# Output projection of a hybrid encoder step: three row tiles in turn, one tile for turned rows, and rows asked for earlier

## The chip, the cores and the metric

One core of one Trainium2 chip runs the whole program. The metric is the time of one execution on the device in microseconds; of several runs the median is given. A profile is one further execution, taken by the hardware profiler.

## The reference, cut to what matters

The program is one inference step of a two-layer encoder over 2048 prompt rows and 32 sample rows of width 1024. The first layer is a gated delta rule, the second attends with shared keys and values. The change lies in the end of the first layer: the output projection, the residual sum and the layer norm.

```python
o = o * lax.rsqrt(jnp.mean(o * o, -1, keepdims=True) + RMS_EPS) * norm_w * jax.nn.silu(z.astype(jnp.float32))
out = o.reshape(b, l, A_VW).astype(x.dtype) @ w_out          # (2080 rows, 1024) @ (1024, 1024)
return layer_norm(DN_ALPHA * x + out, ln_g, ln_b), new_buf, s_new.astype(x.dtype)
```

All of it is computed to float32 accuracy: each operand of a matmul is split into a rounded part and a remainder (`_hi` and `_lo`), and three products are summed.

## The kernel before

**Tiling.** The output projection (`O1.tiles`, with `OutNorm` for the arithmetic) goes over 17 tiles of rows: 14 of 128 prompt rows, the 32 sample rows, and the last two of 128. For each tile the gated output `g` is read turned (128 x 8 x 128), split into `g_hi` (ScalarE, ACT) and `g_lo` (VectorE, DVE), and multiplied by the whole weight matrix, which stays in the on-chip memory as `wo_hi` and `wo_lo`. The two halves of 512 columns are c = 0 (PSUM bank `po`) and c = 1 (bank `ps`). For each half, after 24 matmuls, `add_products` (L1165) computes r = ALPHA * r + bank on DVE, where r holds the tile's 128 rows of the input x, and the statistics for the layer norm follow (L1226).

**The order inside a tile.** `OutNorm.tile` is a generator that stops after every six matmuls, eight times a tile: j = 0 to 3 in the first half, j = 4 to 7 in the second. `O1.tiles` puts work of the tile before, and preparations for the tiles to come, at these stops:

- j = 0: the mean and the inverse root of the tile before (`scaled`, a row of small DVE instructions down to `nb`, L1238);
- j = 1: its normalisation on ACT (L1239), `g_lo` of the next tile (L1209), and the load of `g` for the tile after that (L1187), whose one buffer is free when `g_lo` has been made;
- j = 3: the multiplication by ln_g and the addition of ln_b (L1243, L1244), and the store of the finished rows to the scratch array h (`s_h`, L1261);
- then the first half's update of r from `po`, which is emitted when the generator goes on;
- j = 4: the finished rows of the tile before are turned in blocks of 32 x 32 by DVE (L1267) into a tile `hT`, which four DMAs store to the scratch array (`s_hT`, L1270), each with 1024 pieces of 32 elements;
- j = 6: the load of the next tile's rows of x into r (L1192);
- after j = 7 the second half's update of r, from `ps`.

Between the stops a second generator (`more`) issues work of the next stage: loads of its weights (L1389) and of turned rows (L1367), partial sums on GpSimd (POOL) and their stores (L1432).

**What sets the order.** In this part the order on TensorE (PE), DVE, ACT and SP is that of the program text (`manual_schedule`). All loads and stores named here are issued by SP, one after another; an issue that has to wait holds up the issues behind it. A tile from a pool with two buffers may be written again when the readers of the tile before last are done.

**The buffers that matter.** r comes from the pool `two` of `OutNorm` (two buffers). `hT` comes from the pool `o1_hT` on the right side (two buffers of 128 x 1024 float32), opened when the delta rule is finished; the first tile still takes a buffer of the delta rule. `last.close()` gives that pool back after the last tile, and the next stage's `first_pair` places five tiles of activations (L1412) from there on.

**The next stage** (`P2`) multiplies the normalised rows by the weights of the second layer. Its first seven weight tiles are multiplied singly, in part between the last tiles of the projection; then follow groups of products over partial sums, which need the stored `hT` and the sums.

Of the kernel before, what the change touches and what calls it, by code (L numbers as in the profile page):

```python
# [11 lines left out]
F32 = mybir.dt.float32  # L12
# [9 lines left out]
D = 1024  # L22
# [14 lines left out]
def new_pool(tc, es, name, bufs=1, space=None, side=None):  # L37
    kw = {"reuse_waits": "tile"}
    if side is not None:
        kw["side"] = side  # L40
    if space is not None:
        kw["space"] = space
    return es.enter_context(tc.tile_pool(name=name, bufs=bufs, **kw))
# [1128 lines left out]
class OutNorm:  # L1172
# [15 lines left out]
        return g  # L1188

    def rows(self, src, n):  # L1190
        r = self.two.tile([128, D], F32, tag="r", name="r")
        self.queue.dma_start(r[:n], src)  # L1192
        return r

    spare = None

    def bank(self, c):
        if c and self.spare:
# [48 lines left out]
class O1:  # L1247
# [25 lines left out]
    def tiles(self, tiles, ready, more):  # L1273


        on, last, parts, beside = self.on, None, [], ()
        for t in tiles[:2]:
            while not ready(t):
                yield 1.0
            g = self.fetch(*t)  # L1280
            yield 0.0
            parts.append(on.low(g, on.cast(g, t[2]), t[2]))
        r = self.rows(*tiles[0])
        yield 0.0
        high, coming = None, ()
        for i, t in enumerate(tiles):
            beside = itertools.chain(beside, more(i))
            if i + 1 == len(tiles):
                yield from (out for out in beside if out)
            for j, out in enumerate(on.tile(parts.pop(0), r, t[2])):  # L1290
                yield out
                next(beside, None)
                if j == 0 and last:
                    normalise = on.scaled(*last)
                elif j == 1:
                    if last:
                        normalise()
                    for c in coming:
                        parts.append(on.low(g, high, c[2]))
                    coming = tiles[i + 2:i + 3]  # L1300
                    for c in coming:
                        while not ready(c):
                            yield 1.0
                        g = self.fetch(*c)
                elif j == 3 and last:
                    self.affine(last, *tiles[i - 1])
                elif j == 4 and last:
                    self.turned(last[0], *tiles[i - 1])
                if j == 6 and i + 1 < len(tiles):
                    following = self.rows(*tiles[i + 1])  # L1310
            for c in coming:
                high = on.cast(g, c[2])
            last, r = (r, t[2], on.stats), following
        end = more(len(tiles))
        normalise = on.scaled(*last)
        yield from itertools.islice(end, 2)
        normalise()
        self.affine(last, *tiles[-1])
        yield from itertools.islice(end, 2)
        self.turned(last[0], *tiles[-1])  # L1320
        yield from end


class P2:
# [249 lines left out]
    def plan(self, first, between, late, late_ps):  # L1574


        def singles(tiles, ps):
            return [p for i in tiles for p in self.single(i, ps)]

        one, a = self.groups(0)  # L1580
        two, b = self.groups(1)
        between = singles(between, self.ps)
        last = singles([self.Z + 1], self.ps)
        for n in a:
            self.then(a[n], self.operand(1, a[n].act[1]))
        early = [*singles(first, self.ps), *one, between[0], a["P4"], a["P3"], *between[1:], *two, last[0], b["P4"],
                 b["P3"], last[1]]
        late = singles(late, late_ps)
        self.main = self.stream(early + late, len(early) - 4)
        self.left = 2 * len(early)  # L1590
# [82 lines left out]
    now, later, side, beside = 0, (), iter(()), iter(())  # L1673
# [634 lines left out]
def program(tc, I, O, T, G):  # L2308
    nc = tc.nc
    left, right, mid = ExitStack(), ExitStack(), ExitStack()  # L2310
# [36 lines left out]
    o1 = []  # L2347
# [12 lines left out]
    def outputs():  # L2360
        tiles = [(t * 128, t * 128, min(128, NT - t * 128)) for t in (*range(14), NTT - 1, 14, 15)]
        yield from o1[0].tiles(tiles, lambda t: t[0] in sent, more)
# [27 lines left out]
    front, spare = ExitStack(), ExitStack()  # L2390
    p2.append(P2(tc, right, front, spare, I, O, T, G))
    last = ExitStack()
    hp = new_pool(tc, last, "o1_hT", 2, side="right")
    o1[0].room = lambda: hp.tile([128, KC, 128], F32, tag="hT", name="hT")[:]
    o1[0].on.spare = p2[0].ps
    later = []
# [218 lines left out]
```

## Time and profile before

| | us |
|---|---|
| runs shown (three) | 2056.74, 2059.09, 2065.05 |
| median | 2059.09 |
| profiled execution, whole time | 2061.92 |
| profiled execution, span of the page | 2060.1 |
| output projection in it (loads and tails included), about | 1061 to 1301 |

The span runs from the first instruction to the last; a little more lies around it. Times in the rows are microseconds from the start of the span. Engines: PE = TensorE matmul, PEld = TensorE weight load, DVE = VectorE, ACT = ScalarE, POOL = GpSimd, SP = SyncE (SPq: an issue on its queue). L1165 is line 1165 of the kernel. Matmuls overlap in the records: one lasts 0.39 us and the next begins 0.23 us after it. An idle time in brackets is that of the engine just before the instruction, with what ended it by the profile; a wait for several things is put down to the one that came last.

### The profile page before, as it was taken

How to read it: one execution, taken by the hardware profiler on the slowest of the kernel's cores; microseconds unless marked ns; L12 is line 12 of the kernel's file. 1: busy time of each engine (PE TensorE's matmuls, PEld its weight loads, DVE VectorE, ACT ScalarE, POOL GpSimd, SP SyncE). 2: the span in 40 equal slices, each digit the busy share in tenths (PEclk: the TensorE clock that was granted, in tenths of full speed). 3: DMA queues.
4: the chain of work that ended last, by engine and by line, in shares of the span. 5: the costliest groups of instructions: out<-in, count | busy, mean ns of one | idle time of the engine just before them, and what ended most of it. 6: DMA issues, size and time to landing. Idle time of an engine off the chain costs nothing. (4 is left out here: it accounts for less than half of the span.)

```text
span 2060.1 us, 36519 instructions
## 1 busy us (share of the span) xinstructions
PE 1999.7 (97%) x13246; PEld 1829.3 (89%) x13246; DVE 1477.9 (72%) x2701; ACT 999.0 (48%) x2437; POOL 740.9 (36%) x1151
## 2 busy tenths in 40 slices
PE   8999999999999999999889999899999999999998
PEld 6999999999999989999888887799999997777775
DVE  4677656677665778888987898787777755666665
ACT  4354443436632277777773222533643435555552
POOL 0212112121213258888760114022000014566665
PEclk9999999999999999999999999999999999999999
DMA  5133255447878466665885998888768579433321
GB/s 211 51 124 118 76 125 120 104 103 205 206 168 240 149 207 216 195 202 193 297 281 137 257 247 247 271 270 300 265 196 251 190 218 322 121 103 103 103 74 67
DMA packets 477076, 377.85 MB, mean 183 GB/s; under 512 B 291024, under 2 KB 397808, under 8 KB 476880
## 3 DMA queue, kind: packets, MB, share of 16 engines
q1 hardware_dynamic: 470416, 361.08, 59.4%
q10 hardware_dynamic: 6480, 14.44, 2.0%
q8 instruction: 104, 1.70, 0.3%
q14 instruction: 76, 0.62, 0.1%
HBM read 244.06 MB, written 142.58 MB: 188 GB/s over the span
## 5 line engine op out<-in xcount | busy, mean ns | idle before, releaser
L79 PE MATMUL ps<-act_hi,w_hi 128*128 128x416 f32 x1280 | 455.6, 356 | 3.7 <-DVE z L579 3.7
L81 PE MATMUL ps<-act_hi,w_lo 128*128 128x416 f32 x1280 | 450.5, 353 | 0.0
L80 PE MATMUL ps<-act_lo,w_hi 128*128 128x416 f32 x1280 | 448.8, 351 | 0.0
L79 PEld LDWEIGHTS ps<-act_hi,w_hi 128*128 128x128 f32 x1280 | 240.6, 188 | 8.5 <-DVE z L579 4.0
L81 PEld LDWEIGHTS ps<-act_hi,w_lo 128*128 128x128 f32 x1280 | 240.6, 188 | 3.8
L80 PEld LDWEIGHTS ps<-act_lo,w_hi 128*128 128x128 f32 x1280 | 241.2, 188 | 3.0
L212 DVE SCALAR_TENSOR_TENSOR y<-R,convw,y 128x2083 f32<-128x2083 f32 x72 | 177.7, 2469 | 56.9 <-ACT y L209 52.6
L755 POOL TENSOR_TENSOR tm<-L,Tt 128x60 f32<-128x60 f32 (+19 forms) x365 | 134.9, 370 | 74.4 <-issue 43.2
L56 POOL TENSOR_TENSOR w_lo<-w_raw,w_hi 128x1024 fp32r<-128x1024 f32 x25 | 62.6, 2503 | 273.1 <-ACT w_hi L55 273.1
L1881 ACT ACTIVATE e<-S,nm 128x193 f32<-128x193 f32 (+2 forms) x260 | 104.6, 415 | 102.5 <-DVE nm L1876 61.5
L757 POOL TENSOR_TENSOR Tt<-Tt,tm 128x60 f32<-128x60 f32 (+19 forms) x365 | 139.8, 383 | 28.6
L1895 POOL TENSOR_TENSOR P<-e,sm 128x384 f32<-128x384 f32 (+2 forms) x128 | 102.3, 820 | 119.0 <-DVE sm L1885 113.0
L326 ACT COPY R<-ps 128x416 f32<-128x416 f32 (+1 forms) x144 | 59.6, 445 | 125.5 <-PE ps L81 119.9
L1538 ACT ACTIVATE o<-X 128x416 f32<-128x416 f32 x80 | 41.4, 518 | 151.2 <-PE X L1712 147.8
L1383 POOL TENSOR_TENSOR wo_parts<-wo_parts 128x512 fp32r<-128x512 f32 x16 | 21.6, 1352 | 239.3 <-ACT wo_parts L1699 239.3
L1157 PE MATMUL ot<-wo,g_hi 128*128 128x512 f32 x256 | 103.7, 405 | 0.0
L1158 PE MATMUL ot<-wo,g_hi 128*128 128x512 f32 x256 | 100.8, 394 | 0.0
L1159 PE MATMUL ot<-wo,g_lo 128*128 128x512 f32 x256 | 100.8, 394 | 0.0
L1383 DVE TENSOR_TENSOR w_lo<-w_raw,w_hi 128x512 fp32r<-128x512 f32 x134 | 95.9, 730 | 4.3 <-ACT w_hi L1395 2.6
L1426 POOL TENSOR_TENSOR act_raw<-act_raw 128x416 f32<-128x416 f32 x32 | 41.7, 1303 | 134.1 <-DMA act_raw<-s_hT 132.4
L218 DVE SCALAR_TENSOR_TENSOR y<-th,y 128x2083 f32<-128x2083 f32 x24 | 55.8, 2327 | 31.5 <-ACT th L216 31.5
L1395 ACT CAST w_hi<-w_raw 128x512 fp32r<-128x512 f32 x129 | 76.1, 615 | 1.4 <-PE ps L1711 1.4
(368 smaller groups left out, 5086.8 us busy)
## 6 DMA issues: line engine op xcount, KB each, us to landing
w_raw<-in_b_w SPq DMA_DIRECT2D x60, 512.0 KB
w_raw<-in_w_in SPq DMA_DIRECT2D x40, 512.0 KB
act_raw<-s_hT SPq DMA_DIRECT2D x64, 208.0 KB
s_rows<-o SPq DMA_DIRECT2D x50, 208.0 KB
k<-s_k SPq DMA_DIRECT2D x17, 512.0 KB
E<-s_E SPq DMA_DIRECT2D x17, 512.0 KB
s_hT<-hT SPq DMA_DIRECT2D x65, 128.0 KB
s_bq<-s_rows SPq DMA_DIRECT2D x40, 208.0 KB
```

The lines of the kernel that those rows point to most:

```text
L79: nc.tensor.matmul(ps, hi[:, k, :], xh[:, k, :], start=(k == 0), stop=False)
L80: nc.tensor.matmul(ps, hi[:, k, :], xl[:, k, :], start=False, stop=False)
L81: nc.tensor.matmul(ps, lo[:, k, :], xh[:, k, :], start=False, stop=(k == KC - 1))
L212: nc.vector.scalar_tensor_tensor(out=y[:], in0=R[:, j:j + W], scalar=self.convw[:, i, j:j + 1], in1=y[:], op0=ALU.mult, op1=ALU.add)
L755: P.tensor_tensor(out=tm[:n, i0 - k:, :w], in0=L[:n, i0:, j:j + 1].to_broadcast(sh), in1=Tt[:n, j:j + 1, :w].to_broadcast(sh), op=ALU.mult)
L757: P.tensor_tensor(out=Tt[:n, i0:, :w], in0=Tt[:n, i0:, :w], in1=tm[:n, i0 - k:, :w], op=ALU.subtract)
L1157: nc.tensor.matmul(ps[:n], ghi[:, k, :n], hi, start=a, stop=False)
L1158: nc.tensor.matmul(ps[:n], ghi[:, k, :n], lo, start=False, stop=False)
L1159: nc.tensor.matmul(ps[:n], glo[:, k, :n], hi, start=False, stop=z)
L1383: P.tensor_tensor(out=lo, in0=raw, in1=hi, op=ALU.subtract)
L1881: self.nc.scalar.activation(x.e[:, h, u, :x.n], x.S[:, h, u, :], AF.Exp, bias=x.nm[:, h, u:u + 1], scale=1.0, accum_out=x.sm[:, h, u:u + 1])
L1895: self.nc.gpsimd.tensor_tensor(out=x.P[:, u, :nj * 128].rearrange("r (j h k) -> r j h k", h=2, k=64), in0=x.e[:, :, u, :n].rearrange("r h ...
```

## The change

Three things change, all in `O1.tiles`, `OutNorm.rows` and the pool behind them. The pool `o1_hT` gets one buffer for each kind of tile in place of two for `hT`: one `hT` and, new, one r. From the point where that pool is opened, every third load of rows takes its r from there and the two others from `two` as before, so that three r tiles go round and one `hT` serves all tiles. And with that pool open, the rows of the next tile are asked for at j = 2 in place of j = 6 (or at the first stop after j = 2 where the pool is opened later in a tile).

```diff
--- before.py
+++ after.py
@@ -1188,11 +1188,14 @@
         return g
 
     def rows(self, src, n):
-        r = self.two.tile([128, D], F32, tag="r", name="r")
+        pool = self.third if self.third and self.turn % 3 == 0 else self.two
+        self.turn += bool(self.third)
+        r = pool.tile([128, D], F32, tag="r", name="r")
         self.queue.dma_start(r[:n], src)
         return r
 
-    spare = None
+    spare = third = None
+    turn = 0
 
     def bank(self, c):
         if c and self.spare:
@@ -1282,7 +1285,7 @@
             parts.append(on.low(g, on.cast(g, t[2]), t[2]))
         r = self.rows(*tiles[0])
         yield 0.0
-        high, coming = None, ()
+        high, coming, following = None, (), None
         for i, t in enumerate(tiles):
             beside = itertools.chain(beside, more(i))
             if i + 1 == len(tiles):
@@ -1306,11 +1309,11 @@
                     self.affine(last, *tiles[i - 1])
                 elif j == 4 and last:
                     self.turned(last[0], *tiles[i - 1])
-                if j == 6 and i + 1 < len(tiles):
+                if j >= (2 if on.third else 6) and not following and i + 1 < len(tiles):
                     following = self.rows(*tiles[i + 1])
             for c in coming:
                 high = on.cast(g, c[2])
-            last, r = (r, t[2], on.stats), following
+            last, r, following = (r, t[2], on.stats), following, None
         end = more(len(tiles))
         normalise = on.scaled(*last)
         yield from itertools.islice(end, 2)
@@ -2390,7 +2393,7 @@
     front, spare = ExitStack(), ExitStack()
     p2.append(P2(tc, right, front, spare, I, O, T, G))
     last = ExitStack()
-    hp = new_pool(tc, last, "o1_hT", 2, side="right")
+    o1[0].on.third = hp = new_pool(tc, last, "o1_hT", 1, side="right")
     o1[0].room = lambda: hp.tile([128, KC, 128], F32, tag="hT", name="hT")[:]
     o1[0].on.spare = p2[0].ps
     later = []
```

## Rows read from the trace of the kernel before

**Rows 1.** The page: busy time of PE, and the chain by engine.

```profile
PE 1999.7 (97%) x13246; PEld 1829.3 (89%) x13246; DVE 1477.9 (72%) x2701; ACT 999.0 (48%) x2437; POOL 740.9 (36%) x1151
...
PE 32%; DVE 3%; DMA 2%; issue 1%; ACT 1%; SPq 1%; POOL 0%; DVEq 0%; POOLq 0%; ACTq 0%
```

**Rows 2.** By stage: stretch, length, busy PE, PEld, DVE, ACT, POOL, clock, DMA, GB/s.

```profile
1204.00:1215.00 11.00, 11.00 (x50) 9.13 (x49) 10.16 (x23) 2.30 (x2) 0.00 (x0) 1.00 0.79 197
1215.00:1226.00 11.00, 11.00 (x51) 9.09 (x50) 10.05 (x21) 2.09 (x2) 4.35 (x4) 1.00 0.97 268
...
1248.00:1259.00 11.00, 7.62 (x26) 5.58 (x25) 9.90 (x19) 1.82 (x2) 5.99 (x4) 0.84 0.99 269
...
1281.00:1292.00 11.00, 9.57 (x49) 8.61 (x47) 9.23 (x20) 2.70 (x5) 0.62 (x1) 1.00 0.63 163
1292.00:1303.00 11.00, 9.40 (x47) 8.46 (x46) 7.66 (x12) 4.50 (x10) 0.00 (x0) 1.00 0.60 132
1303.00:1314.00 11.00, 6.97 (x26) 6.08 (x26) 4.33 (x8) 4.59 (x10) 0.00 (x0) 0.84 0.95 333
```

**Rows 3.** Timeline of PE: start, duration, line, operation, tiles, idle time before with releaser.

```profile
1138.23 0.39 PE L1157 MATMUL ps<-wo_hi,g_hi 128*128 128x512 f32 x1
...
1236.15 0.39 PE L1157 MATMUL ps<-wo_hi,g_hi 128*128 128x512 f32 x1
...
1252.98 0.50 PE L1159 MATMUL po<-wo_hi,g_lo 128*128 128x512 f32 x1 [3.38 <-DVE g_lo L1209]
```

**Rows 4.** Timeline of DVE, same columns: updates of r (L1165), g_lo, a transpose.

```profile
1143.86 0.69 DVE L1165 SCALAR_TENSOR_TENSOR r<-r,po 128x512 f32<-128x512 f32 x1 [0.87 <-PE ps L1159]
...
1178.33 0.68 DVE L1165 SCALAR_TENSOR_TENSOR r<-r,po 128x512 f32<-128x512 f32 x1
...
1188.75 0.69 DVE L1165 SCALAR_TENSOR_TENSOR r<-r,po 128x512 f32<-128x512 f32 x1
...
1226.95 1.22 DVE L1209 TENSOR_TENSOR g_lo<-g,g_hi 128x1024 fp32r<-128x1024 f32 x1
...
1231.86 0.69 DVE L1165 SCALAR_TENSOR_TENSOR r<-r,po 128x512 f32<-128x512 f32 x1 [1.02 <-DMA r<-in_x]
...
1233.19 1.23 DVE L1267 STREAM_TRANSPOSE hT<-r 128x1024 f32<-128x1024 f32 x1
...
1244.62 0.69 DVE L1165 SCALAR_TENSOR_TENSOR r<-r,po 128x512 f32<-128x512 f32 x1 [1.54 <-DMA r<-in_x]
```

**Rows 5.** Waits, total, times, longest (us): of 1100 to 1320, 1116 to 1160, 1160 to 1200.

```profile
DVE r L1165 <- DMA r<-in_x: 5.0, 5, 1.5
...
DVE r L1165 <- PE ps L1159: 0.9, 1, 0.9
...
DVE r L1165 <- DMA r<-in_x: 1.4, 1, 1.4
...
DVE r L1165 <- DMA r<-in_x: 0.8, 1, 0.8
```

**Rows 6.** Timeline of SP: loads of r, stores of hT, first loads of the next stage.

```profile
1139.20 0.61 SPq L1192 DMA_DIRECT2D r<-in_x  x1
...
1146.45 5.12 SPq L1270 DMA_DIRECT2D s_hT<-hT  x4
...
1191.33 2.58 SPq L1270 DMA_DIRECT2D s_hT<-hT  x4
...
1226.87 0.61 SPq L1192 DMA_DIRECT2D r<-in_x  x1
...
1234.57 4.83 SPq L1270 DMA_DIRECT2D s_hT<-hT  x4
...
1239.50 0.62 SPq L1192 DMA_DIRECT2D r<-in_x  x1
...
1297.76 4.26 SPq L1412 DMA_DIRECT2D act_raw<-s_hT  x3
```

**Rows 7.** The chain that ended last, in order of time, from 1060 to 1420: start, length, what.

```profile
1296.64 4.50 DMA s_hT<-hT
...
1302.06 3.18 DMA act_raw<-s_sums
...
1336.18 0.45 PE X L1712
```

## The prediction

> **What bounds the kernel now.** The page first: TensorE (PE) is busy 97% of the span, and the chain that ended last runs mostly over PE [rows 1]. So only a stretch in which PE stands still or runs at half clock can give time back. The table by stage finds it: in the output projection PE has no gap in 1204 to 1226, but from 1248 to 1259 it is idle for 3.4 of 11 us at a mean granted clock of 0.84, and it loses 1.4, 1.6 and 4.0 us more in the three later stretches shown, up to 1314 [rows 2]. What ends that first idle time is VectorE (DVE): the matmul after the gap waited 3.38 us for g_lo, which DVE had not got to [rows 3]. So the second half of the stage is paced by DVE, which works in order, and the next view is DVE's timeline.
>
> There a tile takes 10.42 us where nothing disturbs it (updates of r from po at 1178.33 and 1188.75) [rows 4]; PE needs 10.88 us (po complete, and ps begun, at 1138.23 and nine tiles later at 1236.15, so 97.92/9) [rows 3]. DVE could always keep up, but it runs late: the update from po comes 5.6 us after the bank is complete at 1143.86, and 8.5 us after at 1244.62 [rows 3, 4]. The list of waits says why: five updates of r stood still for the load of r from x, 5.0 us together, the longest 1.5; one more, 0.9 us, is put down to a matmul of ps [rows 5]. That one is the update at 1143.86, but it reads po, complete 5.6 us before, and its r was asked for 4.66 us before, as the two others shown were at 4.99 and 5.12 us [rows 4, 6]. I count it among the loads: 5.9 us in six tiles.
>
> Why is r asked for so late? At step j = 6 its issue stands on SP behind the four stores of the previous hT, and those wait for the transpose, which DVE makes late: stores from 1234.57, 4.83 us long, r at 1239.50 [rows 6]. So there is a loop: transpose, stores issued, r issued, r landed, update, transpose. From the transpose at 1233.19 to the update at 1244.62 it took 11.43 us; DVE's own work between the two is 9.09 us (10.42 less the 1.33 from update to transpose, 1231.86 to 1233.19) [rows 4].
>
> **The change part by part.**
>
> (a) r a half tile sooner, in a third tile. At j = 2 its issue stands on SP behind the load of g, which waits for g_lo of the same tile on DVE; in tiles with partial sums up to eight issues stand between. It passes s_h and the four hT stores, which thus go out 0.6 to 0.8 us of SP's time later; POOL's queue isn't touched. Its buffer is that of three tiles ago, whose transpose was one DVE round earlier and whose store to s_h before that, so SP should find it free. From g_lo to the update in the same tile is 4.9 us (1226.95 to 1231.86), and r is used one round after that [rows 4]: 4.9 + 10.42 = 15.3 us for a load that takes 4.7 to 5.1. So the six waits go: minus 5.9 us of DVE time. The number of DMAs, instructions and matmuls stays.
>
> How much of it reaches the end? DVE is 8.5 us late at 1244.62; 5.9 us less leaves 2.6, so no update meets PE instead [rows 3, 4]. After that tile DVE sets the pace up to the last hT: the chain goes from there over the stores of hT (4.50 us to landing) and the loads of the next stage and comes to PE's own pace only at 1336.18 [rows 7]. SP and GpSimd, with the partial sums and those loads, hang on the same DVE steps and shift along. PE can follow: its 3.38 us for g_lo vanish, and its idle time in the four stretches is 10.4 us [rows 2], more than the shift. The half clock after the gap goes too, but PE isn't what ends there, so I give nothing for it.
>
> (b) One hT in place of two. Before, a transpose needed the stores of two tiles ago; now those of the tile before. Behind a waiting transpose stand, on DVE, the update from ps, the statistics and g_lo, and PE's next tile behind those. In a heavy tile: transpose at 1233.19, stores issued until 1239.40; if the last lands 4.50 us after (the one landing that the chain shows), that is 1243.90, and the next transpose, one undisturbed round on, comes at 1243.61 [rows 4, 6, 7]. In a light tile: stores issued until 1193.91, landed by 1198.4; the next transpose is at 1188.75 + 1.33 + 10.42 = 1200.5. So it is free in light tiles and at the edge where the issue of the stores takes about 4 us or more, six tiles of sixteen (up to 5.12; the lightest 2.58) [rows 6]. Bounds of its price: below, zero, since the last store is issued before its piece ends; above, 0.3 us plus the 524 KB of r that now stand ahead of the stores in the queue, 1.9 us at the 269 GB/s of a full stretch [rows 2], so 2.2 us in each of six tiles, 13 us. I take 0.4, near zero: the long pieces are SP held up by a full queue, with earlier stores already moving. A gain is excluded: one buffer can't come free sooner than two.
>
> On this part a rule speaks against the change. The row shows 4.50 us for the landing of a store of hT, which goes out in pieces of 32 elements, and 4.66 to 5.12 for r in rows of 4 KB [rows 4, 6, 7]; so small pieces cost no more there. The Trainium skill, DMA: Bandwidth & Descriptors, section Specifications, puts the smallest transfer for line rate at 512 B, with read-modify-write below that; by it these 128 B pieces would land later where the queue is full, part (b) would sit at its upper end and the sum would be slower than before.
>
> (c) The queue itself. In the four stretches from 1215 to 1259 the DMA engines are 97 to 99% busy, just before that 79% [rows 2]. Pulling the same transfers 5.9 us forward has room for 2.3 us in 1204 to 1215 (0.21 of 11) and at most 1.3 inside the four (0.03 of 44). Missing: between nothing (the waits were only a matter of order) and 5.9 - 3.6 = 2.3 us. I take 0.8, nearer nothing, as 3 of the 5.9 us come before 1170 and DVE keeps its round of 10.42 us after that [rows 4, 5].
>
> (d) Start of the next stage. Its activations are put where hT and the third r were. Before, the first three were issued from 1297.76 on, 4.26 us long, held up until the last hT had landed [rows 6]. With another tile in either place the first ones wait the same or up to two issues (about 0.4 each) more: 0 to 0.8. I take zero, as the load that the chain goes on with stands behind all of them anyway.
>
> Sum: 5.9 - 0.4 - 0.8 = 4.7 us less. The profiled execution took 2061.92 us for a span of 2060.1, 2.8 us above the median of 2059.09; its span would become 2055.4. Against the median: 2054.4.
>
> **The rivals.**
> 1. The queue is the limit, not its order: r lands sooner, and g or hT later by as much. For it: 97% and more from 1215 to 1259. Against it: the undisturbed round between the two heavy stretches, which keeps what the first waits give. With it goes the case that SP can't issue r sooner because its place in memory, given up by the stage before, isn't free. Time: 2057 to 2061, say 2059.
> 2. The single hT becomes the wait. Transpose, stores, landing is then a loop of its own, and it decides where issue and landing together take more than 9.2 us after the transpose's end (10.42 less 1.2). At the upper price that is 13 less 5.9, 7 us slower: 2066. For it: the sum at the edge in six tiles; against it: only six, and PE's two banks hide a delay that comes early.
> 3. More comes back than DVE's waits: PE, with no gap at 1249, keeps its full clock into the next stage, and the idle time there closes as well. The cap is the idle time of 10.4 us: 2049.
>
> **How the numbers follow.** Forecast (a gain of 2.5 to 7 us) 0.60, rival 1 0.22, rival 2 0.11, rival 3 0.07. The three runs of before span 8.3 us, so a median moves by some 2 us either way. The range goes from 2048.5 (rival 3) to 2062.5 (rival 1 with that scatter, and the mild half of rival 2). A measurement of this kernel tells about 0.5%, 10.3 us, from no change: faster than 2048.8 needs rival 3 at its cap or a low median, 0.08; slower than 2069.4 needs rival 2 beyond its price, 0.06; within, 0.86.
>
> **What would show it.** (a) right: no update of r has idle time put down to the load of r, and on SP r stands between g and s_h. (b) right: no idle time before a transpose; wrong: idle time there in tiles with a long piece of stores. (c): the update from po at 1244.62 comes at about 1239.5, and PE's gap of 3.38 us shrinks or goes. The forecast fails if the gap goes and the last hT is stored no sooner, or if DVE stands still before transposes for more than 6 us in all.

## The result, and the profile after

The changed kernel takes 2067.45 us in the median (2064.47 to 2070.41), the one before in the same comparison 2060.81. The ratio is 1.0024 [1.0015, 1.0034]: slower by 5 us (the medians stand 6.6 apart), where 4.7 us less had been forecast. That is under the 0.5% which the prediction names as the bound, but the interval leaves no change out; the time lies 5 us above the range, and the sign is wrong. The profiled execution has a span of 2066.9 us.

The page of the changed kernel, the lines that answer to [rows 1]: the work is the same, but more of the chain lies on DMA and less on PE.

```profile
PE 2002.1 (97%) x13246; PEld 1828.6 (88%) x13246; DVE 1479.6 (72%) x2701; ACT 998.9 (48%) x2437; POOL 741.7 (36%) x1151
...
PE 30%; DMA 5%; DVE 2%; ACT 1%; SPq 1%; issue 1%; POOL 0%; DVEq 0%; ACTq 0%; POOLq 0%
```

The table by stage (columns as in [rows 2]). One more stretch of the kernel before:

```profile
1237.00:1248.00 11.00, 11.00 (x49) 7.12 (x49) 8.20 (x14) 2.71 (x3) 4.76 (x4) 1.00 0.98 258
```

The changed kernel:

```profile
1204.00:1215.00 11.00, 10.74 (x48) 8.54 (x47) 8.84 (x20) 2.74 (x3) 2.18 (x2) 1.00 0.80 192
...
1237.00:1248.00 11.00, 8.88 (x40) 6.42 (x39) 7.16 (x18) 1.55 (x2) 4.29 (x4) 1.00 0.92 258
1248.00:1259.00 11.00, 8.37 (x33) 4.72 (x32) 10.23 (x20) 2.28 (x2) 2.04 (x2) 0.95 1.00 293
```

PE begins to stand still earlier: it already has gaps (0.26 us) in 1204 to 1215, and 2.1 us of them in 1237 to 1248, where there were none. The DMA engines are at 0.92 in 1237 to 1248, where they were at 0.98.

What ends the new gaps is DVE again, now waiting for other things (waits from 1100 to 1320: total, times, longest):

```profile
ACT g_hi L1207 <- DMA g<-s_g: 73.8, 12, 11.9
...
DVE g_lo L1212 <- ACT g_hi L1207: 5.2, 4, 2.1
...
DVE hT L1270 <- DMA s_hT<-hT: 4.1, 4, 1.8
...
DVE g_hi L1212 <- ACT g_hi L1207: 2.4, 1, 2.4
```

None of the waits of r for its load is left; there were 5.9 us of them [rows 5]. In their place DVE waits 5.2 + 2.4 us for g_hi and 4.1 us, before four transposes, for the stores of hT: 11.7 us. ACT, which makes g_hi, itself waits for the load of g, 73.8 us in all; before the change its twelve waits took 58.3 us:

```profile
ACT g_hi L1204 <- DMA g<-s_g: 58.3, 12, 9.4
```

From the first transpose of the stage to the last it is 186.32 us (1112.47 to 1298.79) against 181.13 before (1112.44 to 1293.57): 5.2 us more, of 11.7 - 5.9 = 5.8 that the waits make (DVE's other idle time in the stage fell by 1.3 us, and its busy time grew by 0.6).

DVE's timeline, some of the places (columns as in [rows 4]; the last line is the update that stood at 1244.62 before):

```profile
1168.06 1.25 DVE L1270 STREAM_TRANSPOSE hT<-r 128x1024 f32<-128x1024 f32 x1 [1.83 <-DMA s_hT<-hT]
...
1175.48 1.23 DVE L1212 TENSOR_TENSOR g_lo<-g,g_hi 128x1024 fp32r<-128x1024 f32 x1 [2.06 <-ACT g_hi L1207]
...
1198.17 1.22 DVE L1212 TENSOR_TENSOR g_lo<-g,g_hi 128x1024 fp32r<-128x1024 f32 x1 [1.39 <-ACT g_hi L1207]
...
1245.18 0.60 DVE L1212 TENSOR_TENSOR g_hi<-g,g_hi 128x256 fp32r<-128x256 f32 x1 [2.43 <-ACT g_hi L1207]
...
1248.72 0.68 DVE L1165 SCALAR_TENSOR_TENSOR r<-r,po 128x512 f32<-128x512 f32 x1
```

And PE, with the matmuls that the gaps in 1237 to 1259 stand before (one gap of 3.38 us there in [rows 3]):

```profile
1245.83 0.45 PE L1154 MATMUL po<-wo_hi,g_hi 128*64 128x512 f32 x1 [2.12 <-DVE g_hi L1212]
...
1254.30 0.50 PE L1157 MATMUL po<-wo_hi,g_hi 128*128 128x512 f32 x1 [0.85 <-ACT g_hi L1207]
...
1256.81 0.50 PE L1159 MATMUL po<-wo_hi,g_lo 128*128 128x512 f32 x1 [1.78 <-DVE g_lo L1212]
```

Why g is late is read from SP's timeline. First one tile of the kernel before, from the loads behind the stores of [rows 6] at 1191.33 to the next stores:

```profile
1194.02 0.97 SPq L1192 DMA_DIRECT2D r<-in_x  x1
1195.03 1.17 SPq L1367 DMA_DIRECT2D act_raw<-s_hT  x2
1196.56 0.32 SPq L1187 DMA_DIRECT2D g<-s_g  x1
1199.23 0.32 SPq L1261 DMA_DIRECT2D s_h<-r  x1
1201.70 3.51 SPq L1270 DMA_DIRECT2D s_hT<-hT  x4
```

The same tile in the changed kernel:

```profile
1189.70 0.38 SPq L1187 DMA_DIRECT2D g<-s_g  x1
1190.12 0.43 SPq L1194 DMA_DIRECT2D r<-in_x  x1
1190.65 0.38 SPq L1264 DMA_DIRECT2D s_h<-r  x1
1192.71 7.38 SPq L1273 DMA_DIRECT2D s_hT<-hT  x4
1200.13 1.62 SPq L1370 DMA_DIRECT2D act_raw<-s_hT  x2
1201.85 0.38 SPq L1187 DMA_DIRECT2D g<-s_g  x1
```

Before, r stood behind the stores of hT, then came the loads and g, and SP was idle for 2.3 us before s_h and 2.1 before the next stores: each time it waited for DVE, so it was early. Now g, r and s_h stand together, 1.57 MB asked for within 1.3 us, right ahead of the stores. The four stores take SP 7.38 us in place of 2.58 to 3.51, and g, behind them, is issued only at 1201.85. Its buffer was free at 1199.39, when g_lo of the row at 1198.17 ended.

That distance, from the end of g_lo to the issue of g, is what I call SP's lateness below. Over the eight tiles from the fourth load of the stage to the eleventh it adds up to 4.3 us before (at most 1.5) and to 21.0 us after (1.2 to 4.6 each). From issue to landing (worked out from the times of the semaphores) g takes 5.8 us in the mean of the stage in both kernels, and over these eight tiles 5.78 before and 6.05 after. So in the main it is asked for late; but its landing after the change varies from 4.4 to 7.4 us, and in three of the four tiles where g_lo then waits it took 6.6 to 7.4.

The end of the stage just shifts. The chain, answering to [rows 7]:

```profile
1301.86 4.68 DMA s_hT<-hT
...
1341.27 0.46 PE X L1715
```

The last hT lands at 1306.54, 5.4 us later than before, and PE comes to its own pace at 1341.27, 5.1 us later. SP's first three loads of the next stage took 4.39 us to issue, before 4.26 [rows 6].

### The profile page after: what moved, and what is told of

It reads as the page before. It is cut to its first block, busy times and chain, and to the rows that moved or that the text cites. A ratio compares the mean times of both kernels' runs of the same rounds, so it can differ in the third digit from the quotient of the medians.

```text
span 2066.9 us, 36523 instructions
## 1 busy us (share of the span) xinstructions
PE 2002.1 (97%) x13246; PEld 1828.6 (88%) x13246; DVE 1479.6 (72%) x2701; ACT 998.9 (48%) x2437; POOL 741.7 (36%) x1151
```

## The experiments

Three theories stood against each other. The single hT is the new wait, as rival 2 said. Or it is the place of r in SP's queue, in front of s_h and the stores of hT. Or it is the volume, the same bytes asked for closer together, in whatever queue. In the table, "r" is DVE's waits for r, "g, hT" those for g_hi and for the stores of hT, both from 1100 to 1320; "stores" is the mean time that SP takes to issue the four stores of hT in eleven tiles, from the third of the stage to the thirteenth; "late" is SP's lateness at g, summed over eight tiles; "stage" is the time from the first transpose to the last. All in us, but for the ratio from one profiled execution each; the stage is compared and not the span, as its first transpose already lies anywhere from 1112 to 1117.

| kernel | r | g, hT | stores | late | stage | ratio to before |
|---|---|---|---|---|---|---|
| before | 5.9 | 0 | 3.8 | 4.3 | 181.1 | 1 |
| after | 0 | 11.7 | 6.8 | 21.0 | 186.3 | 1.0024 [1.0015, 1.0034] |
| after, again (e10) | 0 | 10.7 | 6.7 | 19.5 | 185.8 | 1.0020 [1.0005, 1.0036] |
| r at j = 6 (e2) | 5.0 | 1.0 | 3.6 | 3.5 | 181.6 | 0.9997 [0.9988, 1.0006] |
| r behind s_h (e3) | 0 | 5.1 | 5.8 | 16.1 | 179.5 | 0.9997 [0.9988, 1.0007] |
| s_h on ACT (e8) | 0 | 6.2 | 5.8 | 15.6 | 178.0 | 0.9996 [0.9983, 1.0008] |
| r on ACT (e4) | 0.5 | 2.0 | 4.1 | 4.4 | 177.9 | 0.9981 [0.9972, 0.9990] |
| r on ACT, again (e11) | 0 | 1.4 | 3.7 | 1.7 | 178.4 | 0.9983 [0.9970, 0.9996] |
| r on ACT at j = 6 (e7) | 0 | 1.9 | 4.5 | 4.1 | 177.4 | 0.9994 [0.9982, 1.0006] |
| r and s_h on ACT (e9) | 0 | 2.4 | 3.9 | 4.5 | 176.3 | 0.9988 [0.9977, 0.9999] |
| g on ACT (e12) | 0 | 5.0 | 5.0 | 1.2 | 181.4 | 1.0007 [0.9994, 1.0021] |
| before, r on ACT (e5) | 0.2 | 9.9 | 3.9 | 3.3 | 184.6 | 1.0024 [1.0012, 1.0035] |

The column leaves out DVE's waits of another kind, three of which are larger than elsewhere: 1.5 us in e9 before the stage's second transpose, put down to a store of the stage before, and 4.3 and 5.0 us in e12 and e5 at the updates of the sample tile (1.3 to 1.5 in the other kernels). A third r beside two hT was not tried, nor an early r that SP asks for ahead of g.

**r asked for as late as before (e2).** It keeps the third r and the single hT.

```diff
-                if j >= (2 if on.third else 6) and not following and i + 1 < len(tiles):
+                if j >= 6 and not following and i + 1 < len(tiles):
```

> The changed kernel with one part undone: three r tiles and one hT stay, but the rows are asked for at j = 6 again, behind the stores of hT. Theory Q (the place in SP's queue costs: r ahead of s_h and hT holds up the issue of the stores, so g behind them comes late): the long pieces of hT stores (up to 8.4 us) fall back to 2.6 to 5.1 us, DVE waits for g_hi under 2 us in all, but waits for r again for about 5 us; ratio to before 0.999 to 1.001. Theory H (the single hT costs): DVE still stands still before transposes for 4 us or more and the time stays above before, ratio 1.002 to 1.004.

0.9997 [0.9988, 1.0006], 2062.8 us. Its waits, in which no transpose appears:

```profile
DVE r L1165 <- DMA r<-in_x: 3.7, 4, 2.1
...
DVE r L1165 <- DMA act_raw<-s_hT: 1.3, 1, 1.3
...
DVE g_hi L1212 <- ACT g_hi L1207: 1.0, 1, 1.0
```

The stores are back at 2.6 to 4.8 us, but for one set of 6.3. One hT alone costs nothing here, and the waits for r are back (the second line is an update too). The theory of the single hT falls: the transposes of the changed kernel wait because the stores before them are issued slowly.

**r right behind s_h (e3).** Two issues on SP change places, nothing else.

```diff
-                if j >= (2 if on.third else 6) and not following and i + 1 < len(tiles):
+                if j >= (3 if on.third else 6) and not following and i + 1 < len(tiles):
```

> The changed kernel with the rows asked for at j = 3, that is behind s_h and still ahead of the four stores of hT. If it is s_h that must get through before the third store of hT can be issued, and r only harms by standing ahead of s_h: store pieces shrink by the time of r's transfer, some 2 us, and the ratio to before is 0.998 to 1.001. If r harms anywhere ahead of the hT stores: pieces of 5 to 8 us remain, g late as in the changed kernel, ratio 1.002 to 1.005. Theory H (the single hT costs) expects the same as for the changed kernel, 1.002 to 1.004.

0.9997 [0.9988, 1.0007], 2063.77 us.

```profile
DVE g_hi L1212 <- ACT g_hi L1207: 2.1, 1, 2.1
DVE hT L1270 <- DMA s_hT<-hT: 1.7, 2, 0.9
...
DVE g_lo L1212 <- ACT g_hi L1207: 1.3, 2, 0.8
```

The loss goes with the place in front of s_h, but the stores stay long, 4.1 to 7.4 us, and the lateness too: of the first two expectations each has one half met. DVE's waits are 5.1 us, about the 5.9 for r that they replace. What decides is how much of the lateness DVE can take: from the end of one g_lo to the next it has 10.37 - 1.22 = 9.15 us in an undisturbed round, of which landing (5.8 in the mean) and the cast to g_hi (1.05) take 6.85. So some 2.3 us of lateness are free where g lands in its mean time.

The traces bear the sum out tile by tile. In the changed kernel g_lo waited in four of the eight tiles, in e3 in two and in e8 in five. In all eleven, lateness, landing, 0.10 us up to the cast and the cast together are the time from one g_lo to the next within 0.04 us (for the g asked for at 1166.88 in the changed kernel 4.64 + 7.42 + 0.10 + 1.05 = 13.21 of 13.25 us); in the tiles without a wait they are shorter than that time. Lateness and a slow landing count alike: 3.01 us of lateness cost nothing where g landed in 4.4 us, and 2.16 cost 1.39 where it took 7.3.

**r issued by ACT (e4).** All else as in the changed kernel.

```diff
-        self.queue.dma_start(r[:n], src)
+        (self.nc.scalar if self.third else self.queue).dma_start(r[:n], src)
```

> The changed kernel with the rows (from the point where the third tile is there) issued by ACT at the same place of the program, j = 2, in place of SP. Theory Q: SP's queue is free of r, the pieces of hT stores are 2.6 to 5 us, g comes in time, no wait for r: the 5.9 us that the forecast counted come back, ratio 0.997 to 0.999. Theory H: DVE waits before transposes for 4 us or more, ratio 1.000 to 1.003. If it is the DMA engines' time and not the order in SP's queue: ratio 1.000 to 1.002 with g late as well.

0.9981 [0.9972, 0.9990], 2059.91 us against 2063.99: faster than both kernels. SP in the tile shown above, and the waits:

```profile
1191.85 2.86 SPq L1273 DMA_DIRECT2D s_hT<-hT  x4
1194.76 1.52 SPq L1370 DMA_DIRECT2D act_raw<-s_hT  x2
1197.08 0.32 SPq L1187 DMA_DIRECT2D g<-s_g  x1
1199.75 0.32 SPq L1264 DMA_DIRECT2D s_h<-r  x1
1202.22 2.93 SPq L1273 DMA_DIRECT2D s_hT<-hT  x4
```

```profile
DVE g_hi L1212 <- ACT g_hi L1207: 1.3, 1, 1.3
...
DVE hT L1270 <- DMA s_hT<-hT: 0.7, 2, 0.4
DVE r L1165 <- DMA r<-in_x: 0.5, 1, 0.5
```

The order of before is back on SP, without r: stores of 2.86 us, g, a pause, s_h, a pause, stores. Waits of 5.9 us are replaced by 2.5, which leaves 3.4; the stage is 3.3 us shorter, the median 4.1. The same bytes are asked for in the same half tile, so volume alone isn't it.

**The kernel before with r issued by ACT (e5).** Two r, two hT, j = 6.

```diff
-        self.queue.dma_start(r[:n], src)
+        (self.nc.scalar if self.spare else self.queue).dma_start(r[:n], src)
```

> The kernel before with one change: rows are issued by ACT, still at j = 6 and with two r tiles and two hT. ACT then waits for the store of s_h that frees the tile, ahead of its cast of g_hi. If the order in SP's queue is what makes r late in the kernel before: DVE's waits for r (5.9 us) go, ratio 0.997 to 0.999. If ACT's own wait then makes g_hi late: DVE waits for g_hi in place of r, ratio 0.999 to 1.003.

1.0024 [1.0012, 1.0035], 2069.29 us: the waits for r go, as the first expectation said, and the second one's wait for g_hi comes in their place.

```profile
ACT g_hi L1204 <- DMA s_h<-r: 47.9, 5, 12.0
...
DVE g_lo L1209 <- ACT g_hi L1204: 8.3, 4, 4.0
...
DVE g_hi L1209 <- ACT g_hi L1204: 1.6, 1, 1.6
```

With two r the load on ACT must wait until the other buffer's s_h is through, and g_hi is queued behind it on ACT. So the other queue alone isn't the gain: it needs the third r, whose issue finds its buffer free.

**r issued by ACT, but at j = 6 (e7).** The edits of e4 and e2 together.

> The changed kernel with the third r tile and one hT tile, the next rows issued by ACT in place of SP, but only at j = 6 as before. Theory Q (it matters which queue the issue of r stands in, and in front of what, and not how early it is made): the rows then stand behind neither s_h nor the stores of hT, and ACT waits for nothing there, as the third tile has long been free; no update waits for r, and the ratio to the kernel before is 0.997 to 0.9995, as with the early issue on ACT (0.998). Theory E (the half tile of lead is what brings the gain on ACT): the updates wait for r again as in the kernel before, 4 to 6 us in all, and the ratio is 0.9995 to 1.001.

0.9994 [0.9982, 1.0006], 2059.66 us. The ratio doesn't tell the two theories apart, their ranges meet inside the interval. The trace does: no update waits for r, SP's lateness is that of before, and the stage is 3.7 us shorter than before, as short as in e4. The half tile of lead isn't needed; the ratio leaves open whether it is worth the rest of e4's gain.

**s_h issued by ACT, r on SP at j = 2 (e8).**

```diff
-        self.nc.sync.dma_start(self.T["h"][row:row + n, :], last[0][:n])
+        (self.nc.scalar if self.on.third else self.nc.sync).dma_start(self.T["h"][row:row + n, :], last[0][:n])
```

> The changed kernel with r asked for by SP at j = 2, but the store s_h issued by ACT in place of SP. Theory Q (in the changed kernel the stores of hT are held in SP's queue till s_h, behind r, is through, and g goes out late after them): with s_h in the other queue the stores of hT come back to 2.5 to 5 us, DVE waits under 2 us for hT and under 4 for g_hi, and the ratio is 0.997 to 1.000. Its rival, volume: the same bytes are asked for in the same half tile in any queue, the pieces of hT stay at 7 to 8 us and the ratio at 1.001 to 1.004. A third outcome: ACT, which waits at s_h for the affine step of DVE, makes g_hi late as when it waited for a buffer of r (12 us each time there), and the ratio is over 1.004.

0.9996 [0.9983, 1.0008], 2060.33 us. Neither expectation was met as a whole: the loss is gone, as Q said, but the stores stay at 4.3 to 7.7 us, as its rival said (3.3 us of DVE's waits at g_lo, 1.9 at the sample tile, 1.0 at hT). The burst stands on two queues:

```profile
1155.68 0.33 ACTq L1264 DMA_DIRECT2D s_h<-r  x1
...
1155.97 0.43 SPq L1194 DMA_DIRECT2D r<-in_x  x1
1158.15 6.80 SPq L1273 DMA_DIRECT2D s_hT<-hT  x4
```

So the length of the stores follows what is asked for just ahead of them, by either queue; 0.5 MB of r and 0.5 MB of s_h within 0.3 us do it here. The lateness is 15.6 us in all, as in e3, and like there the loss is gone: 6.2 us of waits stand for the 5.9 of before. The stage is 3.1 us shorter than before, though the waits of the table say 0.3 longer: all of DVE's idle time in it is 1.25 us less (19.73 against 20.98), and its busy time 1.87 us less (158.28 against 160.15). 1.4 us of the 3.1 lie in two shorter rounds at the very end. Why DVE's work ran shorter no run shows, and the ratio doesn't show a gain.

**Both r and s_h issued by ACT (e9).** The edits of e4 and e8 together.

> The changed kernel with both r (at j = 2) and s_h issued by ACT, so that SP keeps g, the stores of hT and the loads of the next stage. Theory Q: as r on ACT alone (ratio 0.998) or a little better, 0.996 to 0.999, unless ACT's wait for the affine step makes g_hi late. Rival, volume: what r on ACT alone gained is all there is, s_h changes nothing, 0.9975 to 0.999; if ACT's wait decides, over 1.000 and DVE waits for g_hi more than 8 us in all.

0.9988 [0.9977, 0.9999], 2057.52 us against 2061.17. Stores and lateness as in e4; moving s_h as well brings nothing that can be told.

**g issued by ACT (e12).** r stays on SP at j = 2, in front of s_h.

```diff
-        self.queue.dma_start(g[:, :, :n], src)
+        (self.nc.scalar if self.third else self.queue).dma_start(g[:, :, :n], src)
```

> The changed kernel, r asked for by SP at j = 2 and s_h stored by SP, but the load of g issued by ACT. In the changed kernel SP comes to the load of g 1.2 to 4.6 us after g_lo has freed its buffer, because it is held at the stores of hT; before the change it came 0.0 to 1.5 us after. Theory G (this lateness of g is what makes the changed kernel slow): the pieces of hT stay long, at 5 to 8 us, but g is issued within 0.5 us of g_lo, DVE waits under 3 us for g_hi in place of 7.6, and the ratio to the kernel before is 0.998 to 1.000. Its rival, held stores (the transposes waiting for hT, and the bytes asked for close together, are what costs): the ratio stays at 1.001 to 1.004 with g issued early. A third outcome: ACT, waiting for g_lo at the issue, is late for other work; then it is over 1.004.

1.0007 [0.9994, 1.0021], 2064.16 us. What became of it at the sample tile (DVE's timeline), and ACT's issue of g ahead of it:

```profile
1242.75 0.43 DVE L1212 TENSOR_TENSOR g_hi<-g,g_hi 128x256 fp32r<-128x256 f32 x1 [3.50 <-ACT g_hi L1207]
...
1262.37 0.68 DVE L1169 TENSOR_TENSOR r<-r,g_lo 32x512 f32<-32x512 f32 x1 [3.64 <-ACT g_lo L1168]
```

```profile
1233.32 0.65 ACTq L1187 DMA_DIRECT2D g<-s_g  x1
```

In the middle of the stage theory G is met: g is issued 0.02 to 0.04 us after g_lo (1.0 once), no g_lo waits, and from the fifth tile to the ninth the rounds from transpose to transpose are 10.36 to 10.38 us, where the changed kernel has 12.30, 13.01, 10.39, 11.58 and 12.48. But the stores shrank too (3.7 to 4.9 us in those tiles), as g no longer stands ahead of them on SP, so it doesn't show whether late g or slow stores would cost more alone. At the sample tile it gives the gain back: the issue at 1233.32 stands on ACT 3.8 us after g_lo, and later ACT's copy of the sample rows comes late behind another issue of g, and DVE waits 3.64 us; those two rounds take 14.21 and 16.06 us (12.88 and 14.07 in the changed kernel). That is the third outcome, at one place.

**The changed kernel and e4 a second time, side by side (e10, e11).**

> The changed kernel a second time, unaltered: 1.0015 to 1.0035 of the kernel before, as the first time, with about 12 us of waits of DVE for g_hi and for the stores of hT.

> The changed kernel with r issued by ACT at j = 2, a second time, beside the changed kernel and the one before in the same call. If what the first time showed holds: 0.997 to 0.999 of the kernel before, and 6 to 9 us less than the changed kernel. If it was the scatter of a few runs: 0.999 to 1.000, with the DVE round as even as the first time.

1.0020 [1.0005, 1.0036] and 0.9983 [0.9970, 0.9996], 2067.67 and 2059.24 us beside 2063.73: both as the first time, with 10.7 and 1.4 us of DVE's waits. r on ACT takes 8.4 us off the changed kernel.

## Why the prediction was wrong, point by point

**(a) The six waits go: right in itself.** No update waits for r, and r stands between g and s_h on SP, as said. The step that failed is what stands beside it: r "passes s_h and the four hT stores, which thus go out 0.6 to 0.8 us of SP's time later". That counted the time of r's own issue, and not what r's bytes do to the issue of the stores behind it. A row for more was there, stores of 4.83 us at 1234.57 where light tiles took 2.58 [rows 6], and in the trace of before g and s_h stand right ahead of them:

```profile
1232.57 0.56 SPq L1187 DMA_DIRECT2D g<-s_g  x1
1233.23 1.25 SPq L1261 DMA_DIRECT2D s_h<-r  x1
```

A third DMA in that place adds 524 KB: by estimate 1.57 MB at the 268 GB/s of [rows 2] take 5.9 us to drain, and SP stands at the stores meanwhile. The stores' issue grew from 3.8 to 6.8 us in the mean: the term was 3.0 us a tile, not 0.7. And the sum has no term for what is queued behind the stores on SP, the loads of turned rows and g; the price lay there, 7.6 of the 11.7 us.

**(b) One hT: the price of 0.4 right for the part alone, wrong for the two parts together.** e2 has no wait before a transpose, e4 0.7 and e11 0.5 us; with r ahead of the stores it is 4.1 (3.8 the second time), inside the bounds of 0 to 13. The edge was seen: the wait decides "where issue and landing together take more than 9.2 us". The stores issued from 1157.03 for 8.36 us are past it with any landing over 0.84 us, and the transpose at 1168.06 waited 1.83. On SP, r and s_h right ahead of these stores:

```profile
1155.12 0.43 SPq L1194 DMA_DIRECT2D r<-in_x  x1
1155.65 0.60 SPq L1264 DMA_DIRECT2D s_h<-r  x1
1157.03 8.36 SPq L1273 DMA_DIRECT2D s_hT<-hT  x4
```

The 0.4 came from rows in which r wasn't ahead; r's 524 KB stood only in the upper bound, as 1.9 us. On the rule weighed there (the Trainium skill, DMA: Bandwidth & Descriptors, Specifications, 512 B as the least for line rate): the prediction's "small pieces cost no more there" is a misreading, as it sets 4.50 us for a store of 131 KB beside 4.66 to 5.12 for a load of 524 KB. Asked for one behind the other, stores of hT land 0.78 us apart (median, 168 GB/s) in the kernel before as in the changed one, while r and s_h, in rows of 4 KB, land 1.31 us apart in the changed kernel (400 GB/s). The traces thus agree with the rule, but it isn't what made the change slower: the same pieces in e2, e4 and e11 cost 0 to 0.7 us of waits.

**(c) The queue at 0.8 us (0 to 2.3): wrong step.** It compared shares of busy time with the bytes to be pulled forward. Room on the DMA engines wasn't what was missing: in 1237 to 1248 their share fell from 0.98 to 0.92. The update forecast at 1239.5 came at 1248.72, and in the place of PE's gap of 3.38 us are 2.12, 0.85 and 1.78.

**(d) Start of the next stage at zero: right.** Its loads took as long, and all shifted by 5.1 to 5.4 us.

**The rivals.** Rival 1 had the mechanism (g or hT "later by as much") and was priced at no change, since it was taken as an exchange of one wait for an equal one. It was two for one: 11.7 us of waits for 5.9, since a late stretch of SP met both g and hT. Rival 2 has the time (2066), by luck: its cause, the single hT, is only a part, 4.1 of 11.7 us, and its price had been put at 13. Its "only six" counted tiles of before. Rival 3 did not happen.

**What stays open.** That r in front of s_h and the stores is the cause is shown by e2, e3 and e4, with e10 and e11 as repeats; that DVE feels the late g, by the waits tile by tile. No run separates late g from slow stores, so how the loss splits between them beyond the waits themselves (7.6 and 4.1 us) stays open. e3 and e8, with three quarters of the lateness, lose nothing against the kernel before because their waits, 5.1 and 6.2 us, are about its 5.9; no run changed the slack of 2.3 us by itself.

## What to carry to other kernels

Before a load is asked for sooner, list every issue that it now stands in front of in the same queue, and go on to whatever is queued behind those: the price of the move is the time the queue needs to drain the bytes gathered there, less the slack of what waits behind them, and not the time of one issue. A load whose buffer is surely free, as a third buffer makes it, may go to another engine's queue (4 us gained here); one whose buffer may still be in use takes that engine's other work with it into the wait (e5, e12). Loads and stores spread over the tile were handed over faster than the same bytes in a burst (3.8 against 6.8 us for the stores).

## What the runs showed of the hardware

**A store's issue is held nearly till what is ahead has landed.** With a burst ahead, the first of the four stores of hT (1024 pieces each) is issued in 0.33 us, the second takes 2.05 and the third 5.07 (the tile at 1157.03 of the changed kernel). The third stands until 1164.58, and s_h, the last DMA ahead of it, landed at 1164.84 (worked out from the times of the semaphores). So it is in twelve tiles of that kernel, from the third on: the third store's issue ends 0.11 to 0.30 us before s_h lands. In e3, where r is the last ahead, r takes that place (0.09 to 0.33 us, 0.75 once); in e8, in the tile from 1158.15, the issue ended 0.24 us before r landed. Where s_h had landed sooner, as in three tiles of the kernel before (stores from 1191.33, 1201.70 and 1212.25), the third store took 0.66 to 0.68 us. The full queue is thus read from the length of an issue, and not from the DMA share: in 1237 to 1248, with stores of 6.75 us from 1240.86 on, it was 0.92, lower than before.

**Another engine's queue helped a load that was asked for ahead of the burst, and not a store asked for in it.** In e4 r was asked for by ACT at 1154.48 and landed 4.0 us later, while g, asked for by SP 1.2 us after it, took 6.5 and s_h, 2.9 us after it, 7.6. In e8 s_h was asked for by ACT at 1155.68 and took 8.5 us, as long as r, asked for by SP 0.3 us after it (8.6): up to 1160 ACT's queue moved nothing and SP's 1.15 MB; from 1160 to 1163.5 they moved 0.52 and 0.88 MB side by side. The Trainium skill, DMA: Bandwidth & Descriptors, section Queues, rings and completion order, says that each DMA engine goes round the queues that have work, packet by packet; the stretch from 1160 on agrees with it, the 4 us before it don't, and no run shows what held s_h there. The same page of the Trainium skill says in its section on issuing engines that spreading over them saves only the issuing time, usually a small one; here that time was some 3 us a tile on SP (stores of 6.8 us with r on SP, 4.1 and 3.7 with r on ACT).
